# Feed-forward: the planner starts ahead of TensorE's first product, and VectorE and ScalarE are held to the planned order by edges without semaphores

## The chip, the cores and the metric

The kernel runs on one core of a Trainium2 chip. The metric is the device time of one execution in microseconds (us). Three executions of the kernel before took 1454.38, 1456.62 and 1457.17 us; the median, 1456.62 us, is the time before.

## The reference: what is computed

A two-layer encoder trunk over x (1 x 512 x 1024, float32) and a memory (1 x 256 x 1024). Each layer adds three terms to x: a mixer (layer 0: forgetting and differential attention; layer 1: a chunkwise mLSTM), a cross-attention to the memory, and a gated convolutional feed-forward. The change touches the feed-forward alone:

```python
def conv_ffn(xn, w_up, conv_w, conv_b, w_down):
    h = causal_depthwise_conv(xn @ w_up, conv_w) + conv_b
    g, u = jnp.split(h, 2, axis=-1)
    return (jax.nn.gelu(g) * u) @ w_down

for layer in range(DEPTH):
    ...
    x = x + conv_ffn(rms_norm(x, ffn_norm[layer]), ffn_w_up[layer], ffn_conv_w[layer],
                     ffn_conv_b[layer], ffn_w_down[layer])
```

The feed-forward width is 2816, so `w_up` is 1024 x 5632, and the convolution has three taps.

## The kernel before

**Number format.** Every float32 operand of a product is split into two float32r parts: ScalarE casts the high part (`wh`, `xh`, `ah`, `th`), VectorE subtracts it from the raw value to get the low part (`wl`, `xl`, `al`, `tl`; L279). A product is then three TensorE matmuls, high x high, low x high, high x low (L289 to L291). So each weight slab passes SP (a DMA into `raw`, `dr`, `ra` or `sa`), ScalarE (cast) and VectorE (subtract) before TensorE can use it.

**Feed-forward** (`ffn_steps`). The 5632 columns of `w_up` are 22 pairs p of 128-column blocks, the gate block p and the block 22 + p. TensorE works through p in order:

- `plain(p)`, p = 0 to 4: two blocks of 24 matmuls over 512 columns each, into two of four `acc` banks. VectorE evacuates each with the norm's row factor `rb` (L1321) into the buffer `hs`, of which there are two.
- `seven(p)`, from p = 5: the pair is a 2 x 2 block product made with seven half-size products instead of eight. In order they are p1 (into bank Y), p2 (bank X), p6 (onto Y), p5, p7, p4, p3, each 12 matmuls over 256 columns. Between p1 and p6 ScalarE copies Y aside (`v`, L1394), since p6 adds onto it; p6 therefore waits for `v`. Further copies are `u2` and `u3`. Weight sums are needed too: a load `sa` of half of both blocks, onto which a DMA issued from POOL (GpSimd) adds the second block (`onto`, L1340), and `sb` = half of `sa` plus half of `raw` on VectorE (L1362), later `sb` plus the other half (L1368). Their casts are `s2h` and `s4h`, their low parts `s2l` and `s4l`.
- The matching sums of x (`th`, `tl`, four each) are made once at the start (`forms`, during p = 0 and 1), in the same three `sa` buffers.
- `tail(p)`: conv on ScalarE (L1278, one for each half), two VectorE taps for each half (L1285), gelu (L1293), product (L1295), high cast `ah` (L1299), low part `al`. It works in `c`, which has one buffer: the next pair's conv waits for this pair's `al`.
- `down`: blocks of `w_down` over finished pairs, put as fillers between the seven products; the result is added to x (L512).

At the start TensorE also makes the norm's sums (L1218), VectorE works out the reciprocal root in a chain of small operations (L426 to L432, L441, L446), and TensorE spreads it (L452) into `rb` (L456).

**Order.** `Sched` simulates the feed-forward: each task has an engine, an estimated duration, dependencies, a priority and the buffers it takes and frees, and the task that can start first is emitted next. All clocks start at 0, which is TensorE's first product. The order in which tasks are emitted is the plan. The layer below then orders each engine's instructions once more by its own estimate, keeping data dependencies. Engines execute their queue strictly in order: a waiting instruction holds all behind it. SP's queue holds the loads, and a load waits there until its buffer is free.

Of the kernel before, what the change touches and what calls it, by code (L numbers as in the profile page):

```python
# [66 lines left out]
def folded(ap):  # L67

    return ap.rearrange("p (r k) -> p r k", r=2)


class Item:
    def __init__(self, fn, dur, deps, prio, take, free, chain, pre, after, order, load, st):
        self.fn, self.dur, self.deps, self.prio, self.st = fn, dur, list(deps), prio, st
        self.take, self.free, self.chain, self.pre, self.after = take, free, chain, pre, after
        self.order, self.load = [o for o in order if o is not None], load
        self.ready = None


class Plan:  # L80
# [67 lines left out]
MM = 0.216  # L148


class Task:
    def __init__(self, eng, dur, fn, deps, prio, take, free, lat):
        self.eng, self.dur, self.fn, self.prio, self.lat = eng, dur, fn, prio, lat
        self.deps = [d for d in deps if d is not None]
        self.take, self.free = take, free
        self.end = None


class Sched:
# [2 lines left out]

    def __init__(self, **res):
        self.tasks = []
        self.slots = {r: [0.0] * n for r, n in res.items()}
        self.turn = {r: 0 for r in res}

    def add(self, eng, dur, fn, deps, prio, take=(), free=(), lat=0.25):
        t = Task(eng, dur, fn, deps, prio, take, free, lat)
        t.n = len(self.tasks)  # L170
        self.tasks.append(t)
        return t
# [8 lines left out]
    def run(self):  # L181
        order = sorted(self.tasks, key=lambda t: (t.prio, t.n))
        todo = {}
        want = {r: [] for r in self.slots}
        for t in order:
            todo.setdefault(t.eng, []).append(t)
        for t in self.tasks:
            for r, _ in t.take:
                want[r].append(t)
        now = {e: 0.0 for e in todo}  # L190
        inf = float("inf")
        idle = 0.0
        while any(todo.values()):
            best = None
            for e, ts in todo.items():
                soon, pick = inf, None
                for t in ts[:120]:
                    at = 0.0 if e == "-" else now[e]
                    ok = True
                    for d in t.deps:  # L200
                        if d.end is None:
                            ok = False
                            break
                        at = max(at, d.end + (0.0 if d.eng == e else d.lat))
                    if not ok:
                        continue
                    for r, _ in t.take:
                        if want[r][0] is not t:
                            ok = False
                            break  # L210
                        at = max(at, self.slots[r][self.slot(r)])
                    if not ok or at == inf:
                        continue
                    if at < soon - 1e-6:
                        soon, pick = at, t
                if pick is not None and (best is None or soon < best[0]):
                    best = (soon, e, pick)
            assert best is not None, [(e, t.n, t.prio, [d.n for d in t.deps if d.end is None], t.take) for e, ts in todo.items() for t in ts[:3]]
            at, e, t = best
            todo[e].remove(t)  # L220
            if e == "PE":
                idle += at - now[e]
            t.start, t.end = at, at + t.dur
            now[e] = t.end
            for r, st in t.take:
                want[r].pop(0)
                s = self.slot(r)
                self.turn[r] += 1
# [6 lines left out]
        self.now, self.idle = now, idle  # L235


class Builder:
    def __init__(self, tc, t):
        self.tc, self.nc, self.t = tc, tc.nc, t  # L240
        self.uid = 0
        self.turn4 = 0

# [892 lines left out]
    def ffn_steps(self, layer, mp):  # L1136
# [52 lines left out]
        def block(src, nk, xs, at, bank, deps, steps, tag="raw"):  # L1189
# [14 lines left out]
                last = pe(0.65 * per, fn, [lo, last, *deps], [(bank, st)] if c == 0 else (), [("h", st)] if c == steps - 1 else ())  # L1204
            return st, last

        own = lambda k: (self.xh[k][:], self.xl[k][:])


        def norm():  # L1210
            prev = self.state
            st = {}
            n = {}

            def sums():
                n["ps"] = self.bank("s")
                for i in range(4):
                    nc.tensor.matmul(n["ps"][:, 2 * i : 2 * i + 2], prev["sq"][:, i * P : (i + 1) * P], self.ones2[:], start=True, stop=True)  # L1218

            def root():  # L1220
                self.r = self.rsqrt(n["ps"], 4, 1.0 / DM, EPS)

            def spread():
                self.rb = self.bcast_cols(self.r, SEQ, self.sp, "rb", 1)

            a = pe(0.5, sums, (), [("s", st)])
            b = add("DVE", 2.1, root, [a], a.prio, (), [("s", st)])
# [12 lines left out]
        def forms(k, at):  # L1240

            st = {}
# [593 lines left out]
```

## Time and profile before

| what | value |
|---|---|
| median of three executions | 1456.62 us |
| profiled execution, its own time | 1456.26 us |
| its span, first to last instruction | 1454.5 us |
| TensorE busy | 1423.8 us, 98% |
| VectorE busy | 1177.4 us, 81% |
| ScalarE busy | 826.3 us, 57% |
| POOL busy | 58.7 us, 4% |
| mean DMA rate | 119 GB/s |
| granted TensorE clock, mean | 0.993 |

The profiled execution took 1.8 us more than its span, and 0.36 us less than the median. Times in the rows below are us from the start of the span. In the views, PE is TensorE's matmuls, DVE is VectorE, ACT ScalarE, SPq the loads that SP issues. A row `DVE x <- PE y` of the view of waits says that an engine sat idle before an instruction until another ended. The duration of an instruction overlaps the start of the next one, so what one costs in a queue is read from start to start: 0.60 us for a 128 x 512 subtraction on VectorE, 0.66 us for a tap, 1.13 us for a 128 x 1024 subtraction. The feed-forward of layer 0 runs from about 404 to 700 us, that of layer 1 from about 1105 to 1420 us.

### The profile page before, as it was taken

To read this page: it belongs to the slowest core of one execution; us is meant where nothing else is said; L and a number is where in the kernel's file an instruction comes from. 1 tells how busy PE (TensorE), PEld (TensorE's weight loads), DVE (VectorE), ACT (ScalarE), POOL (GpSimd) and SP (SyncE) were. 2 spreads that over 40 slices of the span, in tenths; PEclk is the share of its full clock that TensorE was granted. 3 is DMA by queue.
4 is the path that set the end of the run, shared out by engine and by line. 5 is a ranking of instruction groups with operands and counts; after the bars stand their busy time and mean duration, and the time that the engine had idled before them with its cause. 6 is when DMAs were issued, how large, how long until landed. Compare 5 with 4: busy or idle time off the path is not lost.

```text
span 1454.5 us, 22322 instructions
## 1 busy us (share of the span) xinstructions
PE 1423.8 (98%) x8366; PEld 1269.8 (87%) x8366; DVE 1177.4 (81%) x2206; ACT 826.3 (57%) x1416; POOL 58.7 (4%) x101
## 2 busy tenths in 40 slices
PE   9999999999998999999999999999999989999998
PEld 7888868899887999999888788889988889999997
DVE  7778886766687999999778868676667889999985
ACT  7767574444464566666456734445445556666654
POOL 0000120000000000000000100000000000000000
PEclk9999999999999999999999999999999999999999
DMA  5222314323236566652232232323323656666412
GB/s 200 88 73 73 102 32 158 117 86 131 87 123 180 150 167 159 169 156 77 84 102 87 73 102 80 109 93 125 116 87 123 174 153 153 174 154 167 124 59 80
DMA packets 61213, 172.55 MB, mean 119 GB/s; under 512 B 6704, under 2 KB 6704, under 8 KB 61104
## 3 DMA queue, kind: packets, MB, share of 16 engines
q1 hardware_dynamic: 55344, 152.69, 31.9%
q0 software_dynamic: 4752, 17.30, 7.0%
q8 instruction: 66, 1.08, 0.3%
q10 hardware_dynamic: 1008, 1.12, 0.2%
q14 instruction: 43, 0.35, 0.1%
HBM read 168.99 MB, written 2.10 MB: 118 GB/s over the span
## 4 chain that ended last, share of the span: by engine, by line
PE 78%; DVE 13%; ACT 4%; issue 3%; DMA 2%; POOL 0%; SPq 0%; DVEq 0%; ACTq 0%; POOLq 0%
PE acc L289 15%; PE acc L291 14%; PE acc L290 14%; PE w L289 5%; PE w L290 5%; PE w L291 5%; DVE wl L279 3%; PE s L289 2%; PE s L290 2%; PE s L291 2%; PE acc L351 2%; PE acc L352 2%; PE acc L353 2%; DVE c L1285 2%; DMA sa<-in_up_dram 1%
## 5 line engine op out<-in xcount | busy, mean ns | idle before, releaser
L289 PE MATMUL acc<-xh,wh 128*128 128x512 f32 (+1 forms) x824 | 289.2, 351 | 0.0
L291 PE MATMUL acc<-xh,wl 128*128 128x512 f32 (+1 forms) x824 | 285.0, 346 | 0.0
L290 PE MATMUL acc<-xl,wh 128*128 128x512 f32 (+1 forms) x824 | 284.8, 346 | 0.0
L279 DVE TENSOR_TENSOR wl<-raw,wh 128x1024 fp32r<-128x1024 f32 (+2 forms) x200 | 239.3, 1196 | 38.2 <-ACT wh L282 35.7
L282 ACT CAST wh<-raw 128x1024 fp32r<-128x1024 f32 (+2 forms) x137 | 140.3, 1026 | 155.2 <-PE acc L290 95.8
L291 PEld LDWEIGHTS acc<-xh,wl 128*128 128x128 f32 x824 | 156.5, 190 | 14.8
L289 PEld LDWEIGHTS acc<-xh,wh 128*128 128x128 f32 x824 | 156.6, 190 | 14.3
L290 PEld LDWEIGHTS acc<-xl,wh 128*128 128x128 f32 x824 | 156.7, 190 | 14.2
L1285 DVE SCALAR_TENSOR_TENSOR c<-hs,vec,c 128x512 f32<-128x512 f32 x176 | 129.2, 746 | 2.7 <-ACT c L1278 2.6
L289 PE MATMUL w<-ah,wh 128*128 128x512 f32 x304 | 115.7, 381 | 0.0
L290 PE MATMUL w<-al,wh 128*128 128x512 f32 x304 | 115.5, 380 | 0.0
L291 PE MATMUL w<-ah,wl 128*128 128x512 f32 x304 | 115.3, 379 | 0.0
L1278 ACT ACTIVATE c<-hs,vec 128x512 f32<-128x512 f32 x88 | 67.5, 809 | 19.1 <-DVE hs L1422 9.3
L291 PEld LDWEIGHTS w<-ah,wl 128*128 128x128 f32 x304 | 57.6, 189 | 8.2
L289 PEld LDWEIGHTS w<-ah,wh 128*128 128x128 f32 x304 | 58.0, 191 | 6.7
L290 PEld LDWEIGHTS w<-al,wh 128*128 128x128 f32 x304 | 57.9, 190 | 6.6
L289 PE MATMUL acc<-mem,wh 128*128 128x256 f32 (+1 forms) x192 | 60.3, 314 | 0.0
L291 PE MATMUL acc<-mem,wl 128*128 128x256 f32 (+1 forms) x192 | 59.7, 311 | 0.0
L1299 ACT CAST ah<-c 128x512 fp32r<-128x512 f32 x44 | 27.2, 619 | 57.0 <-DVE c L1295 56.9
L290 PE MATMUL acc<-mem,wh 128*128 128x256 f32 (+1 forms) x192 | 59.6, 310 | 0.0
L512 DVE TENSOR_TENSOR x<-w,x 128x512 f32<-128x512 f32 x72 | 49.4, 686 | 7.9 <-PE w L291 7.7
L512 DVE TENSOR_TENSOR x<-acc,x 128x512 f32<-128x512 f32 x32 | 22.0, 690 | 40.4 <-PE acc L291 40.4
(373 smaller groups left out, 3810.3 us busy)
## 6 DMA issues: line engine op xcount, KB each, us to landing
raw<-in_up_dram SPq DMA_DIRECT2D x55, 512.0 KB, 3.2
sa<-in_up_dram SPq DMA_DIRECT2D x33, 512.0 KB, 4.2
sa<-in_up_dram POOLq DMA_DIRECT2D x33, 512.0 KB, 5.5
dr<-in_down_dram SPq DMA_DIRECT2D x64, 256.0 KB, 3.6
ra<-in_up_dram SPq DMA_DIRECT2D x33, 256.0 KB, 3.3
raw<-in_xk_dram SPq DMA_DIRECT2D x16, 512.0 KB, 3.2
raw<-in_wo_dram SPq DMA_DIRECT2D x16, 512.0 KB, 3.2
raw<-in_xq_dram SPq DMA_DIRECT2D x16, 512.0 KB, 3.3
```

The lines of the kernel that those rows point to most:

```text
L279: self.nc.vector.tensor_tensor(out=lo, in0=v, in1=hi.bitcast(F32), op=ALU.subtract)
L282: self.nc.scalar.copy(hi, v)
L289: mm(out, wh, xh, start=first, stop=False, skip_group_check=parts)
L290: mm(out, wh, xl, start=False, stop=False, skip_group_check=parts)
L291: mm(out, wl, xh, start=False, stop=last, skip_group_check=parts)
L351: mm(ps, xh[k][:, ts], wh, start=(k == 0), stop=False)
L352: mm(ps, xh[k][:, ts], wl, start=False, stop=False)
L353: mm(ps, xl[k][:, ts], wh, start=False, stop=(k == 7))
L512: self.nc.vector.tensor_tensor(out=x, in0=restored(ps[:]), in1=x, op=ALU.add)
L1278: nc.scalar.activation(st["c_"][:, j, :], hs()[:, j, 2:514], AF.Identity, scale=self.col("cw", (layer * 3 + 2) * 44 + blk), bias=self.col( ...
L1285: nc.vector.scalar_tensor_tensor(out=c, in0=hs()[:, j, n : n + 512], scalar=w, in1=c, op0=ALU.mult, op1=ALU.add)
L1299: nc.scalar.copy(acts[p][0][:], u())
```

## The change

The planner's clocks no longer start at zero for all engines: SP's starts 14 us ahead of TensorE's first product, POOL's 10, ScalarE's and VectorE's 5, and the buffers count as free from 14 us ahead. A task may be given an earliest start (`after`): the norm's sums get 3.4 us, the first of the sums of x 0.8 us. Three empty tasks stand for what VectorE and ScalarE still do for the last block of the cross-attention.

Second, every VectorE and ScalarE instruction of the program now goes through a wrapper (`InOrder`). While the planned feed-forward is emitted, it ties each instruction to the one emitted before it on the same engine with an edge that carries no semaphore and only constrains the order; so the layer below can no longer change the order of these two engines there. TensorE, SP and POOL are not tied. Since the wrapper issues all VectorE and ScalarE instructions, they show line 258 after the change.

```diff
+ORDERED = ("vector", "scalar",)
...
+AHEAD = {"SP": 14.0, "POOL": 10.0, "ACT": 5.0, "DVE": 5.0}
...
-        self.slots = {r: [0.0] * n for r, n in res.items()}
+        self.slots = {r: [-AHEAD["SP"]] * n for r, n in res.items()}
...
-        now = {e: 0.0 for e in todo}
+        now = {e: -AHEAD.get(e, 0.0) for e in todo}
...
-                    at = 0.0 if e == "-" else now[e]
+                    at = max(t.after, -99.0 if e == "-" else now[e])
...
+class InOrder:
+    def __init__(self, tc, engine):
+        self.tc, self.engine = tc, engine
+        self.on, self.next, self.last = False, False, None
+        self.info = mybir.DependencyInfo(mybir.DependencyClass.NoSync, mybir.DependencyReason.SCHED_ONLY)
+
+    def __getattr__(self, name):
+        issue = getattr(self.engine, name)
+
+        def call(*a, **k):
+            i = issue(*a, **k)
+            if self.last is not None and (self.on or self.next):
+                self.tc.add_manual_dep(i.ins, self.last, self.info, reason="planned order")
+            self.last, self.next = i.ins.name, False
+            return i
+
+        return call
...
+class Engines:
+    def __init__(self, tc, names):
+        self.nc = tc.nc
+        self.chains = [InOrder(tc, getattr(tc.nc, n)) for n in names]
...
+    def planned(self, on):
+        for c in self.chains:
+            c.on, c.last = on, None
...
-        self.tc, self.nc, self.t = tc, tc.nc, t
+        self.tc, self.nc, self.t = tc, Engines(tc, ORDERED), t
...
+        X_LAST = 0.8
+        add("DVE", 0.6, None, (), -20.0, after=0.2)
+        add("ACT", 1.2, None, (), -20.0, after=1.0)
+        add("DVE", 1.3, None, (), -20.0, after=1.8)
...
             a = pe(0.5, sums, (), [("s", st)])
+            a.after = 3.4
...
-            a = add("ACT", ACV, lambda: scaled(0), (), at, [("hs", st)])
+            a = add("ACT", ACV, lambda: scaled(0), (), at, [("hs", st)], after=X_LAST)
...
+        nc.planned(True)
         sc.run()
+        nc.planned(False)
```

No instruction is added or removed on any engine; only places in the queues change. Numbers in tile names count allocations, so they differ a little between the two programs; the names ahead of them tell what is what. Three places follow.

**VectorE at the first pair that is made with seven products (p = 5), layer 0.** Before:

```order
L279 TENSOR_TENSOR wl_4640<-raw_4550,wh_4639 128x1024
L1285 SCALAR_TENSOR_TENSOR c_4604<-hs_4260,vec,c_4604 128x512
L1362 TENSOR_TENSOR sb_4689<-sa_4576,raw_4599 128x512
L1295 TENSOR_TENSOR c_4604<-c_4604 128x512
L1362 TENSOR_TENSOR sb_4757<-sa_4578,raw_4619 128x512
L279 TENSOR_TENSOR s2l_4705<-sb_4689,s2h_4704 128x512
L279 TENSOR_TENSOR al_4665<-c_4604,ah_4664 128x512
L1321 TENSOR_TENSOR hs_4261<-acc_950_4626,rb_4305 128x512
L279 TENSOR_TENSOR wl_4682<-raw_4599,wh_4681 128x1024
L1285 SCALAR_TENSOR_TENSOR c_4686<-hs_4261,vec,c_4686 128x512
```

Now:

```order
L258 TENSOR_TENSOR c_4604<-c_4604 128x512
L258 TENSOR_TENSOR hs_4261<-acc_949_4623,rb_4384 128x512
L258 TENSOR_TENSOR al_4665<-c_4604,ah_4664 128x512
L258 TENSOR_TENSOR wl_4681<-raw_4599,wh_4680 128x1024
L258 TENSOR_TENSOR sb_4689<-sa_4576,raw_4599 128x512
L258 SCALAR_TENSOR_TENSOR c_4687<-hs_4261,vec,c_4687 128x512 x2
L258 TENSOR_TENSOR s2l_4705<-sb_4689,s2h_4704 128x512
L258 TENSOR_TENSOR sb_4689<-sb_4689,raw_4599 128x512
L258 TENSOR_TENSOR hs_4260<-acc_956_4667,rb_4384 128x512
L258 SCALAR_TENSOR_TENSOR c_4687<-hs_4261,vec,c_4687 128x512 x2
L258 TENSOR_TENSOR wl_4727<-sa_4576,wh_4726 128x1024
L258 TENSOR_TENSOR c_4687<-c_4687 128x512
```

The first sum `sb` (of `sa_4576`) moved behind the evacuation, `al` and the split of the next slab, four instructions later; the second (of `sa_4578`) moved thirteen later and stands two rows below this piece, ahead of `al` of the pair p = 4.

**ScalarE at the same place, up to the copy `v` of p = 5.** Before:

```order
L1299 CAST ah_4754<-c_4686 128x512
L1278 ACTIVATE c_4777<-hs_4260,vec 128x512
L1183 CAST wh_4773<-dr_4318 128x512
L1278 ACTIVATE c_4777<-hs_4260,vec 128x512
L1394 ACTIVATE v_4793<-acc_974_4759 128x256
```

Now:

```order
L258 CAST ah_4754<-c_4687 128x512
L258 CAST wh_4772<-dr_4272 128x512
L258 ACTIVATE c_4777<-hs_4260,vec 128x512
L258 ACTIVATE v_4793<-acc_974_4759 128x256
L258 CAST wh_4811<-dr_4274 128x512
L258 ACTIVATE c_4777<-hs_4260,vec 128x512
```

One conv instead of two stands ahead of `v`.

**SP's loads ahead of p = 5.** Before:

```order
L1169 DMA raw_4550<-in_up_dram 128x1024
L1169 DMA raw_4599<-in_up_dram 128x1024
L1169 DMA sa_4576<-in_up_dram 128x2x512
L1169 DMA sa_4578<-in_up_dram 128x2x512
L1169 DMA raw_4619<-in_up_dram 128x1024
```

Now:

```order
L1216 DMA raw_4550<-in_up_dram 128x1024
L1216 DMA sa_4576<-in_up_dram 128x2x512
L1216 DMA sa_4578<-in_up_dram 128x2x512
L1216 DMA raw_4599<-in_up_dram 128x1024
L1216 DMA raw_4619<-in_up_dram 128x1024
```

The two `sa` loads moved ahead of a load of `raw`, which waits for a buffer. The same three moves stand at the start of layer 1's feed-forward. Besides, TensorE's four norm sums stand seven matmuls later in each feed-forward; the chain of small VectorE operations behind them now runs on with only one `tl` inside it, and the split `wl` that stood inside it follows behind; and in later pairs most rows move by one to three places, the sums `sb` of two pairs in three by ten.

More of the change, by code (lines that the diff above doesn't have):

```diff
@@ L148, with __init__ @@
 MM = 0.216
+AHEAD = {"SP": 14.0, "POOL": 10.0, "ACT": 5.0, "DVE": 5.0}
 class Task:
-    def __init__(self, eng, dur, fn, deps, prio, take, free, lat):
+    def __init__(self, eng, dur, fn, deps, prio, take, free, lat, after):
+        self.after = after
         self.eng, self.dur, self.fn, self.prio, self.lat = eng, dur, fn, prio, lat
@@ L164, in __init__, with add @@
         self.tasks = []
-        self.slots = {r: [0.0] * n for r, n in res.items()}
+        self.slots = {r: [-AHEAD["SP"]] * n for r, n in res.items()}
         self.turn = {r: 0 for r in res}
-    def add(self, eng, dur, fn, deps, prio, take=(), free=(), lat=0.25):
-        t = Task(eng, dur, fn, deps, prio, take, free, lat)
+    def add(self, eng, dur, fn, deps, prio, take=(), free=(), lat=0.25, after=-99.0):
+        t = Task(eng, dur, fn, deps, prio, take, free, lat, after)
         t.n = len(self.tasks)
@@ L235, in run, with follow, __getattr__ @@
         self.now, self.idle = now, idle
+class InOrder:
[12 more added lines that the diff above has]
+        return call
+    def follow(self):
+        self.next = True
+class Engines:
+    def __init__(self, tc, names):
+        self.nc = tc.nc
+        self.chains = [InOrder(tc, getattr(tc.nc, n)) for n in names]
+        for n, c in zip(names, self.chains):
+            setattr(self, n, c)
+    def __getattr__(self, name):
+        return getattr(self.nc, name)
+    def planned(self, on):
+        for c in self.chains:
+            c.on, c.last = on, None
 class Builder:
     def __init__(self, tc, t):
-        self.tc, self.nc, self.t = tc, tc.nc, t
+        self.tc, self.nc, self.t = tc, Engines(tc, ORDERED), t
         self.uid = 0
```

## The prediction

> **What bounds the kernel now.** I read the page's first part, then TensorE's waits, then the stages by window.
>
> ```profile
> span 1454.5 us, 22322 instructions
> ...
> PE 1423.8 (98%) x8366; PEld 1269.8 (87%) x8366; DVE 1177.4 (81%) x2206; ACT 826.3 (57%) x1416; POOL 58.7 (4%) x101
> ```
>
> TensorE is busy 98% of the span, so a reordering that adds and removes no work can win only what TensorE waits, plus what it runs at a lower clock. Its waits within 404 to 1404 us, which holds both feed-forwards:
>
> ```profile
> PE acc L289 <- ACT v L1394: 13.1, 2, 6.8
> PE acc L289 <- ACT u L1394: 0.7, 2, 0.4
> ...
> PE s L452 <- DVE sqt L446: 0.6, 2, 0.3
> PE s L289 <- DVE hs L1397: 0.5, 2, 0.2
> ```
>
> Two waits for the copy `v`, one in each feed-forward, are 13.1 us; the others are half a microsecond or less at a time. The view by windows (length; busy time of PE, PEld, DVE, ACT, POOL; granted clock; DMA share; GB/s) around them:
>
> ```profile
> 461.00:467.90 6.90, 0.24 (x3) 0.05 (x1) 6.03 (x10) 3.44 (x6) 0.30 (x1) 0.79 0.40 138
> 467.90:471.80 3.90, 3.75 (x15) 3.57 (x16) 3.77 (x7) 2.14 (x5) 0.55 (x1) 0.50 0.69 142
> ...
> 480.00:660.00 180.00, 180.00 (x1356) 172.60 (x1355) 173.53 (x262) 113.05 (x189) 10.25 (x12) 1.00 0.60 160
> ...
> 1162.00:1168.50 6.50, 0.33 (x3) 0.14 (x2) 5.63 (x9) 3.05 (x7) 0.39 (x1) 0.71 0.33 113
> 1168.50:1172.40 3.90, 3.78 (x17) 3.68 (x18) 3.77 (x7) 2.10 (x5) 0.47 (x1) 0.61 0.77 150
> ```
>
> The clock is lowered during each wait and stays low after it: 3.9 us at 0.50, then at 0.61. From 480 to 660 us TensorE never stops, but VectorE is at 173.5 of 180 us; a rival comes from that.
>
> **Why `v` is late.** VectorE in its order of time, layer 0 (the bracket is idle time and what ended it):
>
> ```profile
> 444.43 1.22 DVE L279 TENSOR_TENSOR wl<-raw,wh 128x1024 fp32r<-128x1024 f32 x1
> 445.56 0.75 DVE L1285 SCALAR_TENSOR_TENSOR c<-hs,vec,c 128x512 f32<-128x512 f32 x1
> 450.81 0.69 DVE L1362 TENSOR_TENSOR sb<-sa,raw 128x512 f32<-128x512 f32 x1 [4.50 <-DMA sa<-in_up_dram]
> 451.42 0.69 DVE L1295 TENSOR_TENSOR c<-c 128x512 f32<-128x512 f32 x1
> 454.46 0.69 DVE L1362 TENSOR_TENSOR sb<-sa,raw 128x512 f32<-128x512 f32 x1 [2.35 <-DMA sa<-in_up_dram]
> ...
> 456.27 0.69 DVE L1321 TENSOR_TENSOR hs<-acc,rb 128x512 f32<-128x512 f32 x1
> 456.88 1.22 DVE L279 TENSOR_TENSOR wl<-raw,wh 128x1024 fp32r<-128x1024 f32 x1
> ...
> 459.27 1.41 DVE L1285 SCALAR_TENSOR_TENSOR c<-hs,vec,c 128x512 f32<-128x512 f32 x2
> ...
> 464.96 0.69 DVE L279 TENSOR_TENSOR al<-c,ah 128x512 fp32r<-128x512 f32 x1
> ```
>
> Two sums `sb` stand at the head of VectorE's queue while the DMA that fills `sa` is under way: 4.50 + 2.35 = 6.85 us idle, with evacuation, `al` and taps behind them. ScalarE at that place:
>
> ```profile
> 442.85 1.05 ACT L1183 CAST wh<-raw 128x1024 fp32r<-128x1024 f32 x1 [1.62 <-PE acc L290]
> ...
> 465.69 0.81 ACT L1278 ACTIVATE c<-hs,vec 128x512 f32<-128x512 f32 x1 [0.76 <-DVE al L279]
> 466.41 0.60 ACT L1183 CAST wh<-dr 128x512 fp32r<-128x512 f32 x1
> ...
> 467.64 0.36 ACT L1394 ACTIVATE v<-acc 128x256 f32<-128x256 f32 x1
> ```
>
> and TensorE:
>
> ```profile
> 458.40 0.27 PE L289 MATMUL acc<-xh,wh 128*128 128x256 f32 x1
> ...
> 460.97 0.28 PE L291 MATMUL acc<-xh,wl 128*128 128x256 f32 x1
> 468.05 0.58 PE L289 MATMUL acc<-th,s2h 128*128 128x256 f32 x1 [6.81 <-ACT v L1394]
> ```
>
> p1 begins at 458.40 and is over by about 459.8, so `v` could run from then. It runs at 467.64, since ScalarE has a conv ahead of it that waits for `al` (one buffer `c`), and `al` ends at 465.6, late by VectorE's idle time. Layer 1 shows the same pair of waits:
>
> ```profile
> 1151.21 0.69 DVE L1362 TENSOR_TENSOR sb<-sa,raw 128x512 f32<-128x512 f32 x1 [3.81 <-DMA sa<-in_up_dram]
> ...
> 1155.03 0.69 DVE L1362 TENSOR_TENSOR sb<-sa,raw 128x512 f32<-128x512 f32 x1 [2.52 <-DMA sa<-in_up_dram]
> ```
>
> **The new order, step by step (layer 0).** VectorE's taps end at 445.56 + 0.66 = 446.2 and the product `c` at 446.8. Next is now the evacuation of the bank that TensorE fills as the third block ahead of p1. The cast at 442.85 waited for the end of the block before it, at 442.8; two blocks of 5.2 us lie between 448.0 and 458.40. So VectorE waits for TensorE until about 448.3, 1.5 us that hide under TensorE's own work. From there up to and including `al` the new order has ten 128 x 512 operations (evacuation, `al`, `sb`, `s2l`, `sb` again, evacuation, product, `s4l`, the second `sb`, `al`), four taps and two 128 x 1024 splits: 10 x 0.60 + 4 x 0.66 + 2 x 1.13 = 10.9 us, start to start. That gives `al` by 459.2 instead of 465.6. ScalarE's conv takes 0.72 us more (465.69 to 466.41 above), to 460.0, then `v` 0.4 us, to 460.4. p2 keeps TensorE until about 461.1, so p6 finds `v` ready, 0.7 us ahead. ScalarE's casts in between each have 0.5 us or more, since VectorE has other work before each low part.
>
> Does the first `sb` still wait? In the new order VectorE reaches it after evacuation, `al` and split, 448.3 + 0.60 + 0.60 + 1.13 = 450.6; the data were there at 450.8 before. So the wait is 0.2 us at most even if no transfer gains. The second is reached at 458.0, and its data came at 454.5. The loads should gain too:
>
> ```profile
> 431.68 5.18 SPq L1169 DMA_DIRECT2D raw<-in_up_dram  x2
> 436.96 1.69 SPq L1169 DMA_DIRECT2D sa<-in_up_dram  x2
> ...
> 442.91 1.00 POOL L1340 DMA_DIRECT2D sa<-in_up_dram  x1 [70.58 <-PE acc L290]
> ```
>
> The `sa` loads were issued at 436.96, right behind a `raw` that waited for its buffer; ahead of it they go out once the load of 431.68 and the second `tl` (whose buffer they take) are done, at 433 to 434, some 3 us earlier, and POOL's adding DMA with them. I count that as reserve. What is moved past is one `raw`, whose buffer comes free at 436.5 as before.
>
> Terms: layer 0, the wait 6.81, and 3.9 us at clock 0.50, which cost 3.9 x 0.50 = 1.95; layer 1, 6.3 (13.1 less 6.8) and 3.9 x 0.39 = 1.5. Sum 8.8 + 7.8 = 16.6 us. [...]
>
> Other edits. The norm's sums, seven matmuls later (about 1.5 us), no longer wait for `sq`; the chain behind them runs without splits inside, so the spread waits 0.2 to 0.5 us instead of 0.3: 0, bounds -0.3 and +0.5 in each layer. The split `wl` behind that chain moves from 412.4 to about 415.5, and the block that uses it starts near 422: covered. For `v`'s handoffs between the two engines I take 0.2 in each layer (bounds 0 and 1.5, twice the 0.76 us handoff above).
>
> Rounds with seven products, which are the rest of the feed-forward:
>
> ```profile
> 482.55 1.23 DVE L1422 TENSOR_TENSOR hs<-hs,rb 128x1024 f32<-128x1024 f32 x1
> ...
> 491.00 1.22 DVE L279 TENSOR_TENSOR wl<-raw,wh 128x1024 fp32r<-128x1024 f32 x1
> ...
> 495.78 0.69 DVE L279 TENSOR_TENSOR a22l<-ra,a22h 128x512 fp32r<-128x512 f32 x1 [0.28 <-ACT a22h L1356]
> ...
> 497.10 1.22 DVE L1422 TENSOR_TENSOR hs<-hs,rb 128x1024 f32<-128x1024 f32 x1
> ```
>
> A round is 497.10 - 482.55 = 14.55 us. The split for the next p1 was over at 492.1, and p1 began at 496.37:
>
> ```profile
> 496.37 0.28 PE L289 MATMUL acc<-xh,wh 128*128 128x256 f32 x1
> ```
>
> Its cast now follows `ah` and `u3` on ScalarE: from the end of the product `c` at 491.0, `ah` 0.6, `u3` 0.4, the cast 0.95 and the split 1.13 end at 494.2, about 2 us of margin instead of 4. Then come the split of `sa` (1.13) and the addition to x (0.60): 495.9, where `a22l` starts, as before, because the `dr` split ahead of it now follows the row at 497.10. So the round keeps its phase. Cost 0; above, 0.3 us a round, VectorE's spare time being (180 - 173.5) / 12.4 = 0.5 us a round.
>
> Sum: 1456.26 - 16.6 + 0.4 = 1440.1 us for the profiled execution; the median of before lies 0.36 higher, so **1440.5 us**.
>
> **Rivals.**
>
> *A wait for `v` remains* in both layers, about 3.5 us each, because an input of the ten operations comes late: a handoff, or POOL's DMA. For it: the margin is only 0.7 us. Against: the count above leaves VectorE no data wait over 0.2 us. Of the gain 16.6, 7.0 stays, and about 1 of slower clock: 1456.6 - 8.6 = 1448. [...]
>
> *The adding DMA lands later.* [...] From rows: it landed 7.9 us after its issue (442.91 to 450.8) with VectorE idle for 4.5 of them; in the rounds the page's median for it is
>
> ```profile
> sa<-in_up_dram POOLq DMA_DIRECT2D x33, 512.0 KB, 5.5
> ```
>
> with VectorE 96% busy. That speaks against it. A landing 4 us later would make `v` about 3.5 us late in each layer: 1448 again.
>
> *VectorE becomes the bound in the rounds* (slower). Strict order at 96% load: if the planned order makes VectorE idle s more than its spare time in each round, the 33 rounds lose 33 s less about 2 us of margin in each layer. It outweighs 16.6 from s = (16.6 + 4) / 33 = 0.62; at 0.75 us, one handoff as above in each round, the time is 1440 + 24.8 - 4 = 1461. For it: rounds were free of TensorE waits before, and two thirds of the sums `sb` move by ten places. Against: the phase worked out above holds, and `sb` has a round to spare.
>
> *The change does nothing*, because the layer below had the plan's order already: 1456.6. The rows in order show otherwise.
>
> **How the numbers follow.** Forecast 0.70 (own range 1438.5 to 1444); a wait remains 0.11; the adding DMA later 0.02; VectorE bound 0.10, of which 0.08 slower than before and 0.02 between; no effect 0.03; the rest, faster by a little, 0.04. About 0.2% (2.9 us) is what a measurement of this kernel can tell from no change. Faster 0.88, same 0.04, slower 0.08. The range 1437.5 to 1450 takes in the first three.
>
> **What would show it.** Right: no wait of TensorE for `v` over 1 us, clock 1.00 in both starts, VectorE idle about 1.5 us ahead of an evacuation near 448 and not at `sb`. Wrong: `v` still ending a wait near 461, a VectorE row that waits for the DMA of `sa`, or TensorE waiting for `wh`, `wl` or `s4l` in the rounds.

## The result and the profile after

| | before | after |
|---|---|---|
| executions, us | 1454.38, 1455.06, 1456.62, 1457.17 | 1441.61, 1441.76, 1442.09, 1442.36 |
| median, us | 1455.84 | 1441.92 |
| span of the profiled execution, us | 1454.5 | 1440.6 |

The ratio is 0.9905, 95% interval 0.9888 to 0.9922: 13.9 us faster, where 16.2 was forecast against the profiled execution; the median lies 1.4 us above the 1440.5 forecast, inside its range. In a second measurement the same pair gave 1440.92 and 1456.25, ratio 0.9897 [0.9882, 0.9912].

The page of the changed kernel, first part (every VectorE and ScalarE instruction now shows line 258; the product's three matmuls, L289 to L291 before, are L336 to L338):

```profile
span 1440.6 us, 22255 instructions
...
PE 1421.0 (99%) x8366; PEld 1266.6 (88%) x8366; DVE 1185.4 (82%) x2206; ACT 820.4 (57%) x1416; POOL 59.2 (4%) x101
```

TensorE does the same 8366 matmuls in a span shorter by 13.9 us. What it waits for within 404 to 1390 us, which holds the feed-forward of layer 0 and most of that of layer 1 (total, times, longest):

```profile
PE s L499 <- DVE sqt L258: 1.1, 4, 0.3
PE acc L336 <- ACT v L258: 1.0, 2, 0.7
...
PE acc L336 <- ACT u L258: 0.6, 2, 0.3
```

The 13.1 us of waiting for `v` are 1.0. The windows around the place of the old stall, and the rounds (same columns as in the prediction):

```profile
461.10:462.10 1.00, 0.34 (x4) 0.14 (x3) 1.00 (x3) 1.00 (x3) 0.00 (x0) 1.00 0.12 45
462.10:466.00 3.90, 3.90 (x24) 3.61 (x25) 3.83 (x8) 2.56 (x5) 0.86 (x1) 1.00 0.73 151
480.00:660.00 180.00, 180.00 (x1352) 172.44 (x1351) 174.53 (x259) 108.87 (x188) 9.41 (x11) 1.00 0.58 155
```

The 3.9 us behind the stall, at clock 0.50 before, run at 1.00. VectorE in its order of time, layer 0:

```profile
448.38 0.69 DVE L258 TENSOR_TENSOR c<-c 128x512 f32<-128x512 f32 x1 [0.46 <-DVE c L258]
448.99 0.68 DVE L258 TENSOR_TENSOR hs<-acc,rb 128x512 f32<-128x512 f32 x1
449.76 0.69 DVE L258 TENSOR_TENSOR al<-c,ah 128x512 fp32r<-128x512 f32 x1
450.71 1.23 DVE L258 TENSOR_TENSOR wl<-raw,wh 128x1024 fp32r<-128x1024 f32 x1 [0.25 <-ACT wh L258]
451.85 0.68 DVE L258 TENSOR_TENSOR sb<-sa,raw 128x512 f32<-128x512 f32 x1
452.45 1.53 DVE L258 SCALAR_TENSOR_TENSOR c<-hs,vec,c 128x512 f32<-128x512 f32 x2
453.90 0.69 DVE L258 TENSOR_TENSOR s2l<-sb,s2h 128x512 fp32r<-128x512 f32 x1
454.62 0.69 DVE L258 TENSOR_TENSOR sb<-sb,raw 128x512 f32<-128x512 f32 x1
...
459.62 0.69 DVE L258 TENSOR_TENSOR sb<-sa,raw 128x512 f32<-128x512 f32 x1
460.22 0.69 DVE L258 TENSOR_TENSOR al<-c,ah 128x512 fp32r<-128x512 f32 x1
```

Neither sum `sb` (451.85 and 459.62) has a bracket: 4.50 and 2.35 us of idle time are gone, and `al` starts at 460.22 instead of 464.96, although the feed-forward begins 0.36 us later in this profile. ScalarE and TensorE at the same place:

```profile
460.94 0.81 ACT L258 ACTIVATE c<-hs,vec 128x512 f32<-128x512 f32 x1 [0.67 <-DVE al L258]
461.66 0.36 ACT L258 ACTIVATE v<-acc 128x256 f32<-128x256 f32 x1
```

```profile
461.14 0.28 PE L338 MATMUL acc<-xh,wl 128*128 128x256 f32 x1
462.08 0.38 PE L336 MATMUL acc<-th,s2h 128*128 128x256 f32 x1 [0.67 <-ACT v L258]
```

The chain is the old one, `al`, conv, `v`, p6, only shorter. It still ends 0.83 us too late (462.08 less 461.14, less the 0.11 us from one such matmul to the next).

Since both kernels issue the same matmuls, the time between the starts of two matmuls, counted by their place in TensorE's queue, compares stages free of everything outside. "Start" is from a mark eight matmuls ahead of the feed-forward's first one (402.83 us before, 403.19 after) to the last of p2, "v" from there to p6, "rounds" from p6 on, "end" the last pairs of layer 1 and the finish (in layer 0 the end is within the rounds):

| stage, us | layer 0 before | after | layer 1 before | after |
|---|---|---|---|---|
| start | 58.13 | 57.95 | 58.14 | 57.95 |
| v | 7.08 | 0.94 | 6.56 | 0.59 |
| rounds | 230.13 | 228.29 | 194.82 | 193.40 |
| end | | | 84.36 | 85.43 |

The sum is 639.2 before and 624.5 after: 14.7 us. A second profile of the changed kernel gave the same four stages within 0.02 us each. Whole executions are less steady. In the attention of layer 0, which no version touches, the profile of the changed kernel has a stretch of half clock:

```profile
195.17:198.58 3.41, 1.65 (x12) 1.04 (x11) 3.33 (x9) 3.32 (x6) 0.11 (x1) 1.00 0.02 5
198.58:201.99 3.41, 3.41 (x7) 1.30 (x7) 1.66 (x11) 1.99 (x8) 1.38 (x3) 0.50 0.00 0
```

Five profiles have it (before, both of the change, the edges alone, the larger dose), nine do not; the same 15 matmuls take 5.4 to 5.5 us there in the five and 3.9 in the nine. So where two versions differ by a microsecond, the stages are compared below, and the times stand beside them.

### The profile page after: what moved, and what is told of

Its sections match the earlier page's. It is cut to its first block, busy times and chain, and to the rows that moved or that the text cites. A ratio compares the mean times of both kernels' runs of the same rounds, so it can differ in the third digit from the quotient of the medians.

```text
span 1440.6 us, 22255 instructions
## 1 busy us (share of the span) xinstructions
PE 1421.0 (99%) x8366; PEld 1266.6 (88%) x8366; DVE 1185.4 (82%) x2206; ACT 820.4 (57%) x1416; POOL 59.2 (4%) x101
## 4 chain that ended last, share of the span: by engine, by line
PE 78%; DVE 14%; ACT 3%; issue 3%; DMA 0%; POOL 0%; SPq 0%; DVEq 0%; ACTq 0%; POOLq 0%
PE acc L336 15%; PE acc L337 15%; PE acc L338 15%; PE w L338 5%; PE w L336 5%; PE w L337 5%; DVE wl L258 3%; PE s L336 2%; PE s L337 2%; PE s L338 2%; DVE c L258 2%; PE acc L398 2%; PE acc L399 2%; PE acc L400 2%; DVE x L258 1%
## 5 line engine op out<-in xcount | busy, mean ns | idle before, releaser
L258 ACT CAST wh<-raw 128x1024 fp32r<-128x1024 f32 (+2 forms) x200 | 204.2, 1023 | 192.6 <-PE acc L337 120.1
L336 PE MATMUL acc<-xh,wh 128*128 128x512 f32 (+1 forms) x824 | 289.4, 351 | 0.0
L338 PE MATMUL acc<-xh,wl 128*128 128x512 f32 (+1 forms) x824 | 284.8, 346 | 0.0
L338 PEld LDWEIGHTS acc<-xh,wl 128*128 128x128 f32 x824 | 156.5, 190 | 14.8
L336 PEld LDWEIGHTS acc<-xh,wh 128*128 128x128 f32 x824 | 156.6, 190 | 14.2
L338 PE MATMUL w<-ah,wl 128*128 128x512 f32 x304 | 115.4, 380 | 0.2
L336 PE MATMUL w<-ah,wh 128*128 128x512 f32 x304 | 115.4, 380 | 0.0
L258 ACT ACTIVATE c<-hs,vec 128x512 f32<-128x512 f32 x88 | 71.0, 810 | 26.8 <-DVE hs L258 22.6
L258 DVE TENSOR_TENSOR x<-acc,x 128x512 f32<-128x512 f32 (+1 forms) x43 | 28.1, 654 | 51.1 <-PE acc L338 51.0
L338 PEld LDWEIGHTS w<-ah,wl 128*128 128x128 f32 x304 | 57.5, 189 | 9.0 <-DVE wl L258 1.0
L336 PEld LDWEIGHTS w<-ah,wh 128*128 128x128 f32 x304 | 57.6, 190 | 6.6
L336 PE MATMUL acc<-mem,wh 128*128 128x256 f32 (+1 forms) x192 | 60.3, 314 | 0.0
L338 PE MATMUL acc<-mem,wl 128*128 128x256 f32 (+1 forms) x192 | 59.7, 311 | 0.0
## 6 DMA issues: line engine op xcount, KB each, us to landing
raw<-in_up_dram SPq DMA_DIRECT2D x55, 512.0 KB, 3.3
sa<-in_up_dram SPq DMA_DIRECT2D x33, 512.0 KB, 4.5
sa<-in_up_dram POOLq DMA_DIRECT2D x33, 512.0 KB, 5.5
raw<-in_xk_dram SPq DMA_DIRECT2D x16, 512.0 KB, 3.2
raw<-in_wo_dram SPq DMA_DIRECT2D x16, 512.0 KB, 3.2
raw<-in_xq_dram SPq DMA_DIRECT2D x16, 512.0 KB, 3.3
```

The costliest lines, as they stand in the source:

```text
L258: i = issue(*a, **k)
L336: mm(out, wh, xh, start=first, stop=False, skip_group_check=parts)
L338: mm(out, wl, xh, start=False, stop=last, skip_group_check=parts)
```

## The experiments

### Late sums with the old loads, and old sums with early loads

The change does two things at the old stall: it moves the two sums `sb` back in VectorE's queue, and SP issues the loads of `sa` earlier. The first two kernels undo one each, the third leaves all edges out.

Loads late: the two loads are emitted behind the `raw` again and tied there.

```diff
...
+            held = b1 if p < 7 else None
...
+            if p == 5:
+                self.behind = [l2.fn]
+                l2.fn = lambda fs=self.behind: [f() for f in fs]
+            if held:
+                self.behind.append(held.fn)
+                held.fn = None
```

> The changed kernel with one thing undone: at the first pair of the seven products the two loads of sa are issued behind the raw again, as in the kernel before (in the trace of before their added data landed at 450.79 and 454.44 us, in that of the change at 445.85 and 451.44). Order on VectorE and ScalarE is that of the change. Theory (VectorE's order alone takes the wait away): the first sum sb is reached at 451.85 and the second at 459.62, later than 450.8 and 454.4, so neither waits: 1441.9 us, within 0.7 of the change, TensorE's waits for v 0.5 to 0.8 us in each layer as in the change. Rival (the earlier loads are what helped): VectorE or the cast of sa waits for the landing again and v is late by some 3 us or more in each layer: 1448 or more.

Measured 1441.75 us, ratio to before 0.9900 [0.9885, 0.9915]. Waits for `v`, and VectorE at the two sums:

```profile
PE acc L336 <- ACT v L258: 2.3, 2, 1.3
```

```profile
450.99 0.69 DVE L258 TENSOR_TENSOR sb<-sa,raw 128x512 f32<-128x512 f32 x1 [0.55 <-DMA sa<-in_up_dram]
...
458.77 0.68 DVE L258 TENSOR_TENSOR sb<-sa,raw 128x512 f32<-128x512 f32 x1
```

The first sum now waits 0.55 us for the DMA, and the waits for `v` grow from 1.0 to 2.3 us in both layers together; the granted clock has a mean of 0.999. The theory was 0.7 us off in each layer and right in the main: with the old loads the new place of the sums wins nearly all. The earlier loads are worth 1.3 us of TensorE's time in the two layers.

Sums early: back at their old place, loads early as in the change.

```diff
-            b2 = add("DVE", tt(512), s2_, [b1, l2], at - 5.0, [("sb", sb)])
+            AT = {5: 41.9, 6: 42.6}
+            b2 = add("DVE", tt(512), s2_, () if p in AT else [b1, l2], at - 5.0, [("sb", sb)], after=AT.get(p, -99.0))
```

> The changed kernel with the first two sums sb put back where the kernel before had them, behind the product c and ahead of al and the evacuation; loads early as in the change. Theory (a sum at the head of VectorE's queue holds what stands behind it until its data land): the first is reached at about 449.0 and its data were there at 445.85; the second is reached at 449.6 and its data land at 451.44, so VectorE idles 1.9 us, al ends some 1.6 us later, TensorE waits 2.4 us for v in layer 0 and about 2 in layer 1 instead of 0.83 and 0.48: 1445 us (1444 to 1447). Rival (with early loads the place of the sums does not matter): 1441.9 within 0.5, waits for v as in the change.

Measured 1448.08 us (1444.83 to 1448.99), ratio 0.9944 [0.9928, 0.9961]. The profiled execution is the fastest, 1444.83:

```profile
PE acc L336 <- ACT v L258: 4.2, 2, 3.3
```

```profile
446.77 0.69 DVE L258 TENSOR_TENSOR sb<-sa,raw 128x512 f32<-128x512 f32 x1
449.81 0.69 DVE L258 TENSOR_TENSOR sb<-sa,raw 128x512 f32<-128x512 f32 x1 [2.36 <-DMA sa<-in_up_dram]
```

```profile
458.50:461.90 3.40, 0.69 (x7) 0.50 (x5) 3.37 (x7) 1.68 (x3) 0.00 (x0) 1.00 0.48 154
461.90:465.30 3.40, 2.80 (x13) 2.81 (x14) 3.37 (x7) 2.40 (x5) 0.86 (x1) 0.51 0.51 112
```

A sum at the head of the queue blocks again, 2.36 us, and passes it on to `v`. In layer 1 the second sum waits only 0.27 us at the same place, and the stage "v" takes 1.14 us there against 3.58 in layer 0, where 2 us of waiting were expected in layer 1 too: the old place costs time only where the data are late. In layer 0 the half clock is back for 3.4 us. The median is 1 us above the range expected: the other three executions were 2.9 to 4.2 us longer, at mean clocks of 0.996 and 0.997 against 0.998, which fits more half clock in them; they were not profiled.

### The planner ahead, without edges

```diff
-ORDERED = ("vector", "scalar",)
+ORDERED = ()
```

> The planner starts ahead of TensorE's first product, but no engine is tied to its order: the loads of sa go out early, while the sums sb stay where they were in the kernel before, at the head of VectorE's queue. Theory: the second sum is reached at about 448.4 and its data land at 451.4, 3 us idle instead of 6.85; TensorE waits for v some 3.3 us in each layer: 1441.9 + 5 = 1447 if the clock stays up, 1452 if it is halved for the same 6.8 us in both layers. Rival 1 (only the order matters, the loads are nothing): 1456 within 1. Rival 2 (the planner's earlier start is all of the gain): 1442 within 1.

Measured 1442.16 us (1441.39 to 1445.21), ratio 0.9905 [0.9891, 0.9920]: the change's own ratio, without a single edge.

```profile
PE acc L336 <- ACT v L1446: 3.0, 2, 1.9
```

```profile
445.83 0.68 DVE L1414 TENSOR_TENSOR sb<-sa,raw 128x512 f32<-128x512 f32 x1
...
447.83 0.69 DVE L1414 TENSOR_TENSOR sb<-sa,raw 128x512 f32<-128x512 f32 x1 [0.71 <-issue]
```

```profile
434.73 1.00 POOL L1392 DMA_DIRECT2D sa<-in_up_dram  x1 [64.04 <-DVE c L1337]
438.57 0.86 POOL L1392 DMA_DIRECT2D sa<-in_up_dram  x1 [2.84 <-DVE al L326]
```

Before, the second of these was

```profile
444.22 0.86 POOL L1340 DMA_DIRECT2D sa<-in_up_dram  x1 [0.31 <-DVE c L1285]
```

My theory missed by 5 us, and the second rival was right. The sums stand at the head of the queue as in the kernel before, and yet they hardly wait, since POOL issues the adding DMAs at 434.7 and 438.6, counted from the mark of the stages (401.2 here, 402.8 before) 6.5 and 4.0 us earlier than before (442.91 and 444.22). In the change and in the kernel with the sums early these two come only 3.3 and 2.0 us earlier. So the data of the second sum land 44.8 us behind the mark without edges, 48.3 in the change, 48.8 with the sums early and 51.6 before, and the old place of the sums costs time in the one kernel and not in the other. Why POOL is earlier without edges is not shown. By stages it is 13.4 us better than before, and 1.3 behind the change: 2.1 more at `v`, 1.1 less at the end of layer 1.

### The edges, without the planner ahead

```diff
-AHEAD = {"SP": 14.0, "POOL": 10.0, "ACT": 5.0, "DVE": 5.0}
+AHEAD = {"SP": 0.0}
...
-        add("DVE", 0.6, None, (), -20.0, after=0.2)
-        add("ACT", 1.2, None, (), -20.0, after=1.0)
-        add("DVE", 1.3, None, (), -20.0, after=1.8)
...
-            a.after = 3.4
```

> VectorE and ScalarE tied to the plan, but the planner starts all engines at zero as in the kernel before (no earliest starts, no empty tasks). VectorE's order at the first two sums sb is the same as in the change; the norm's operations and the sums of x at the start of the feed-forward stand elsewhere (up to 44 places on TensorE). Theory (the edges are the gain, the earlier start only shapes the norm part): TensorE's waits for v at most 1 us, no half clock, 1442 within 2. Rival (without the earlier start the plan's order fits the chip badly): new waits of TensorE in the first 20 us of the feed-forward, 1446 or more.

Measured 1465.64 us, ratio 1.0062 [1.0047, 1.0077]: slower than before. No wait for `v` is among TensorE's long ones; three long ones stand in both layers:

```profile
PE s L499 <- DVE sqt L258: 8.1, 4, 3.8
PE s L1266 <- DVE sq L258: 5.9, 2, 2.9
PE acc L336 <- ACT wh L258: 5.1, 2, 2.6
```

ScalarE shows why (its order of time):

```profile
414.17 0.58 ACT L258 COPY rb<-s 128x512 f32<-128x512 f32 x1 [7.18 <-PE s L499]
414.65 1.05 ACT L258 CAST th<-sa 128x1024 fp32r<-128x1024 f32 x1
415.60 2.94 ACT L258 CAST wh<-raw 128x1024 fp32r<-128x1024 f32 x3
```

Two rows of ScalarE at the same place in the kernel before:

```profile
411.08 1.04 ACT L1183 CAST wh<-raw 128x1024 fp32r<-128x1024 f32 x1
416.73 0.58 ACT L456 COPY rb<-s 128x512 f32<-128x512 f32 x1 [4.61 <-PE s L452]
```

A plan that starts all engines with TensorE's first product puts the norm ahead of the first weight casts, and the edges hold ScalarE to that: it is idle for 7.18 us with four casts behind it. In the kernel before, casts of `wh` at 399.4, 404.5 and 411.1 us all stand ahead of `rb` at 416.7. The start takes 70 and 71 us up to and with `v`, against 65.2 and 64.7 before; part of it is half clock, 10.2 us of it in layer 0 and 13.7 us in layer 1. The edges are no gain by themselves: they need a plan that knows how early the engines are free, while that plan does not need them.

### One engine tied, the other not

```diff
-ORDERED = ("vector", "scalar",)
+ORDERED = ("vector",)
```

and `("scalar",)` in the second.

> The changed kernel with edges on VectorE alone; ScalarE's order is left to the layer below (267 of its instructions stand up to 3 places from the change). Loads and VectorE's order as in the change. Theory (what counts is when VectorE gets past the first two sums): 1442 within 1, TensorE's waits for v under 1.5 us in each layer. Rival (ScalarE's order, a conv ahead of the copy v, decides): v comes 3 us or more late in each layer, 1448 or more.

> The planner starts ahead, edges on ScalarE alone. VectorE is left to the layer below, which puts the first two sums sb at the head of its queue as before, and SP's loads of sa stand behind the raw as before. So both of the things that by themselves gave the whole gain (late sums with the old loads: 1441.8; early loads with the old sums: 1442.2) are missing. Theory (either is enough, one is needed): TensorE waits 6 us or more for v in both layers, clock halved behind it: 1456 within 2. Rival (there is a third way, the planner's early start or ScalarE's order): 1448 or less.

VectorE alone: 1447.12 us, ratio 0.9934 [0.9919, 0.9949]. ScalarE alone: 1462.0 us, ratio 1.0038 [1.0025, 1.0051]. TensorE's waits in the first, then in the second:

```profile
PE acc L336 <- ACT u L1446: 3.2, 8, 0.9
PE acc L336 <- ACT v L1446: 2.5, 2, 1.3
```

```profile
PE acc L336 <- ACT v L258: 13.0, 2, 6.5
PE acc L336 <- ACT u L258: 4.3, 3, 2.0
```

At `v` both came out as expected: it hangs on VectorE, not on ScalarE's order. Both were too slow, by 5 and 6 us, for the most part from a cause that neither theory had: waits for the copies `u` in the rounds and at the end, 3.2 and 4.3 us in total, which the kernels with both engines tied or with none tied do not have (0.6 and 0.7). Rounds and end together grow from 507.1 us to 512.0 with VectorE alone and to 514.6 with ScalarE alone; with none tied they take 506.1. The 514.6 also hold the half clock behind the stall at `v`, as the 509.3 of the kernel before do, so against that kernel ScalarE's order alone costs 5.3. The engines hand each other work many times a round; I take it that one in a planned order and one in another order wait for each other, but no run tests this by itself. ScalarE alone shows one thing more: the planner starts ahead there too, and yet SP issues the loads of `sa` at 436.89, as late as before (436.96).

### Strict order where it pays

Edges up to plan time 75 us, which covers the start and the first pair of seven products (the wrapper is switched off from there on):

```diff
+            if self.gate:
+                self.gate(t.start < 75.0)
...
+        def gate(on):
+            if on != seen[0]:
+                seen[0] = on
+                nc.planned(on)
```

> The changed kernel with edges only up to plan time 75 us (norm, plain pairs, first pair of seven products); rounds and the end are ordered by the layer below. Theory (all of the gain comes at the start, the strict order in the rounds costs and brings nothing): 1441.9 within 0.7, TensorE's waits after 480 us into each layer as in the kernel before. Rival 1 (strict order in the rounds or at the end of layer 1 costs the 1.4 us by which the change fell short there): 1440.5. Rival 2 (it brings something there): 1443 or more.

The second sum behind `al`:

```diff
-            b2 = add("DVE", tt(512), s2_, [b1, l2], at - 5.0, [("sb", sb)])
+            AT = {6: 57.0}
+            b2 = add("DVE", tt(512), s2_, [b1, l2], at - 5.0, [("sb", sb)], after=AT.get(p, -99.0))
```

> The changed kernel with the second sum sb moved 7 places further back, behind al; nothing else moves. In the change TensorE still waits 0.83 us for v in layer 0 and 0.48 in layer 1, and the second sum is one of the ten operations ahead of al, 0.60 us each. Theory: al and v come 0.6 us earlier, the waits shrink to about 0.2 and 0: 1440.9 (1440.4 to 1441.5). Rival (the sum is needed soon after, or v hangs on something else): 1441.9 or more, with a wait for s2l or s2h in the next round.

Both in one, beside the changed kernel on one chip:

> Edges only up to plan time 75 us, and the second sum sb moved 7 places further back, behind al: the two versions that measured 1439.5 and 1440.8 in one. Theory (strict order in the rounds costs 1.4 us, and the second sum 0.4 in each layer; without strict order in the rounds nothing gives the 0.4 back): 1438.7, some 2.5 to 3 us below the change measured beside it. Rival (the rounds' waits for hs come back because the sum is late for them): 1439.5 or more.

> The changed kernel itself, beside the other three on one chip, as their base. Expected 1441.9 within 0.7. In the profiled execution shown first, TensorE lost about 1.7 us in the attention of layer 0 (198 to 202 us, code that the change does not touch) which the later kernels' profiles do not show; if that was chance, this one may come out up to 1.7 us lower.

| kernel | median, us | ratio to before | start and v, two layers | rounds | end |
|---|---|---|---|---|---|
| the change, again | 1440.92 | 0.9897 [0.9882, 0.9912] | 117.4 | 421.7 | 85.4 |
| edges at the start only | 1439.51 | 0.9883 [0.9869, 0.9898] | 117.4 | 421.8 | 84.4 |
| second sum late | 1440.80 | 0.9891 [0.9875, 0.9908] | 116.6 | 422.4 | 85.5 |
| both | 1439.48 | 0.9888 [0.9875, 0.9902] | 116.6 | 422.3 | 84.4 |

The medians of the second and third row were measured beside other executions of the kernel before than the first and fourth; the ratios and the stages compare all four. The edges behind the start cost 1.1 us at the end of layer 1 and do nothing in the rounds: the theory that all stays as it is (1441.9) missed, and the first rival (1440.5) was nearer. The later second sum wins 0.8 us at `v`, near the 1.1 expected, but the rounds give 0.5 to 0.7 of it back, so "both" is not the 1438.7 expected. By stages it is the best, 623.3 us against 624.5 of the change; the intervals of the ratios overlap. The half clock in the attention showed again in the profile of the repeated change; its other three executions, not profiled, had spans 0.9 to 1.9 us shorter.

### A dose of VectorE work

```diff
-            acted[p] = add("DVE", tt(512), lambda: self.sub(acts[p][1][:], u(), acts[p][0][:]), [h], at + 9.0, (), [("c", st)])
+            acted[p] = add("DVE", tt(512), lambda: [self.sub(acts[p][1][:], u(), acts[p][0][:]) for _ in range(5 if p == 4 else 1)], [h], at + 9.0, (), [("c", st)])
```

> A dose: the changed kernel with the low part al of pair 4 computed five times instead of once (the same values), 4 x 0.60 = 2.4 us more on VectorE just ahead of v's conv in each layer. TensorE's wait for v should grow from 0.83 and 0.48 us to 3.2 and 2.9. [...] Rival (clock loss in proportion to the wait, 3.5 us for 13.1 us of waiting before): 6.1 us, with a lowered clock in each layer.

> The same with al of pair 4 computed eight times: 7 x 0.60 = 4.2 us more, waits for v of 5.0 and 4.7 us. [...] Rival (in proportion): 8.4 + 2.2 = 10.6 us. If the clock stays up: 8.4.

Measured 1445.62 us, ratio 0.9932 [0.9919, 0.9944], and, with eight `al` in place of five, 1450.93 us, ratio 0.9966 [0.9953, 0.9978], beside 1440.92 for the change. I had put the dose in the wrong place: the `al` ahead of v's conv is that of pair 3 (the text on the change has it as that of p = 4, which is wrong), and `v` did not move (0.83 and 0.48 us lost, as in the change). The dose fell into the first round instead, so it is luck that the smaller one came out 4.7 us over the change, where twice the 2.4 us reckoned make 4.8, and the larger one 10.0 where a rival had 10.6. The question on `v` was not asked, but two others got an answer. First, the first round has hardly any margin for VectorE. The smaller dose in layer 0:

```profile
466.35 3.59 DVE L258 TENSOR_TENSOR al<-c,ah 128x512 fp32r<-128x512 f32 x5
469.86 0.68 DVE L258 TENSOR_TENSOR sb<-sb,raw 128x512 f32<-128x512 f32 x1
```

Five `al` take 3.51 us from start to start where one takes 0.60, so the dose was 2.9 us and not the 2.4 reckoned, and the larger one 5.1 and not 4.2. In each layer 2.9 us more made the rounds 2.76 and 2.69 us longer, 5.1 us made them 4.92 and 4.86 longer. Second, the clock. In the larger dose TensorE waits for the same thing for the same time in both layers:

```profile
PE acc L338 <- DVE wl L258: 4.1, 2, 2.0
```

```profile
471.10:474.50 3.40, 2.28 (x19) 2.04 (x17) 3.30 (x6) 1.23 (x3) 0.00 (x0) 1.00 0.00 0
474.50:477.90 3.40, 2.48 (x22) 2.48 (x23) 3.40 (x5) 0.51 (x1) 0.00 (x0) 1.00 0.42 135
1170.90:1174.30 3.40, 1.41 (x12) 1.42 (x13) 3.40 (x6) 0.00 (x0) 0.00 (x0) 1.00 0.14 31
1174.30:1177.70 3.40, 3.40 (x18) 3.40 (x17) 3.29 (x6) 1.00 (x2) 0.00 (x0) 0.50 0.79 251
```

In layer 1 a half clock of 3.4 us follows; in layer 0 there is none. It cost nothing on balance here, since the rounds grew alike in both layers: in layer 0 TensorE waits another 1.2 us for a copy `u` further on, which in layer 1 it does not. The stretches are laid in steps of 3.413 us from the start of the half clock: in layer 1 the wait falls into one step, with TensorE busy for 1.41 of 3.40 us; in layer 0 it lies across two, busy for 2.28 and 2.48.

## Why the prediction held, and where it did not

**What VectorE's order does.** Right. The chain `sb`, `al`, conv, `v`, p6 was the bound: moving the sums alone takes the wait away (late loads: 1441.75), putting them back brings a part of it back (early sums: 4.2 of the 13.1 us, 1448.08), and ScalarE's order alone leaves it at 13.0 us.

**The earlier loads.** "I count that as reserve." Right for the changed kernel, where without them 1.3 us are lost, and too small a view of the change: the earlier start of the planner is a second remedy, whole by itself (1442.16 without edges). The forecast took the edges for the means and the planner's start for their companion; the runs show either remedy to suffice, the edges alone to be harmful, and the start alone to be enough. What the start does for `v` it does by the loads, and they follow it only if the layer below puts them early: with ScalarE alone tied they stayed late, and the wait was 13.0 us. In the changed kernel they went out at 434.83 us, 2.1 us earlier than before and not some 3.

**The term for `v`.** Forecast 6.81 + 6.3 less 0.4 for handoffs, 12.7; measured 7.08 + 6.56 less 0.94 and 0.59, 12.1. "p6 finds `v` ready, 0.7 us ahead" is the step that failed: `al` started at 460.22 where the count gives 458.6 (459.2 less its own 0.60). Of these 1.6 us, 0.7 is the evacuation, which began at 448.99 and not at 448.3: VectorE came to it late from its own queue, and the wait of 1.5 us for TensorE did not exist (TensorE's own last matmul of p2 was 0.17 us later too, 461.14 against 460.97). The rest, 0.9, is in the run from there: two short waits (`al` starts 0.77 and the split 0.95 us behind the operation ahead of them, instead of 0.60 each), twice 0.13 for a pair of taps of which the second reads the first (1.45 us from start to start, 2 x 0.66 reckoned), and 0.12 at the sum that overwrites what `s2l` reads.

**The clock.** Forecast 1.95 + 1.5 = 3.45; measured 1.84 + 1.42 = 3.26, the difference in the rounds, which would also hold what the new order costs or wins there. Right. A wait well under the 6.81 us of before can have half clock behind it too: in the larger dose one of 2.0 us in layer 1, with TensorE busy for 1.41 of 3.40 us, was followed by 3.4 us at 0.50 (which cost nothing on balance), and one of 2.0 us in layer 0 was not. In the change the clock stayed at 1.00 behind the waits of 0.83 and 0.48 us, and they did cost only themselves.

**Norm edits.** Forecast 0 with bounds -0.3 and +0.5 a layer; measured -0.18 and -0.19.

**Rounds.** "Cost 0" was right for the rounds and wrong for the end of layer 1, which the forecast did not look at: +1.07 us there with edges, none without. No later pair is left there to fill TensorE's waits, which I take to be why the order shows at this place and not in the rounds. The rival's "about 2 us of margin" that would soften a late VectorE was not there in the first round, as the dose shows; later rounds were not tried.

**Sum.** Forecast -16.2, measured by stages -14.7: 0.6 at `v`, 0.2 at the clock and 1.07 at the end short, 0.37 gained at the norm. The gain at the norm lay within the bounds but was not forecast, and hides a part of what fell short. The two spans differ by 13.9 and not 14.7, because the rest of the program took 0.8 us longer in the profile of the change.

**Rivals.** A remaining wait was there, but of 0.8 and 0.5 us and not 3.5. The adding DMA did not land later: the two that feed the sums landed 5.9 and 8.9 us after POOL issued them, against 7.9 and 10.2 before. For all transfers into `sa` between 425 and 460 us, SP's among them, the view of the tile gives, against 5.3, 6.9 and 10.2 before,

```profile
DMA to landing us min/median/max: 3.2/5.9/8.9
```

with VectorE busy for 10.64 us of the 11.50 from 440.00 on, in which the two that feed the sums landed; before, it was busy for 4.75 of the 11.60 from 442.90 on. VectorE did not become the bound in the rounds: TensorE is busy for all of the 180 us from 480 to 660.

## What to carry to other kernels

A queue that runs strictly in order should not have an operation at its head whose data are still on their way (4.50 and 2.35 us of idle VectorE before): either move the operation back or the transfer forward, and try each by itself, because two remedies in one change hide which of them is needed. An imposed order is only as good as the plan's picture of when each engine is free; impose it where the layer below goes wrong, on all engines that hand work to each other there, and leave the rest alone. A wait of TensorE can cost more than itself: behind the one of 6.81 us in the kernel before, TensorE worked for 3.9 us at a granted clock of 0.50.

## What the runs showed of the hardware

- Half clock came in stretches of 3.4, 6.8, 10.2 or 13.7 us ahead of the last microseconds of the profiles. In the kernel before they start at 198.72, 464.96 and 1164.69 us and last 3.413, 6.827 and 6.827 us; the starts are 266.24 and 699.73 us apart, 78 and 205 times 3.413. In the 3.4 us ahead of one TensorE was busy for 0.69 (early sums, from 458.50), 1.41 (larger dose, from 1170.90) and 1.65 us (the attention, after, from 195.17); in the edges alone 1.78 us were followed by full clock:

```profile
403.21:406.62 3.41, 1.78 (x9) 1.21 (x7) 0.81 (x2) 0.87 (x2) 0.00 (x0) 1.00 0.00 0
406.62:410.03 3.41, 1.05 (x8) 0.97 (x8) 2.12 (x9) 0.37 (x1) 0.00 (x0) 1.00 0.00 0
```

  So there was half clock behind 3.4 us in which TensorE had been busy for as much as 1.65. Nearly the same idle time did not always end so: without edges TensorE was busy for 1.74 of the 3.50 us from 194.50, and the clock stayed at 1.00; in the change it was busy for 1.74 of the 3.50 us from 195.10, with 0.50 behind it. What decides between the two no run shows. The half clock in the attention cost 1.5 us in the five profiles that have it, and the other nine have none there, which I take to be a part of the spread of the executions.
- In the change 83 of 84 neighbouring taps on VectorE start 0.78 us apart, in the kernel before 25 of 27 start 0.66 apart, 0.12 us less; I put the difference down to a tap that reads the result of the one right ahead of it: the planned order keeps the two taps of a half together, and I read the pairs at 0.66 as taps of different halves, which the rows do not name. Repeats of `al`, which write the same tile, start 0.72 us apart instead of 0.60. For the same 2206 instructions VectorE was busy 1185.4 us in the change and 1177.4 before.
